# Feed-forward down-projection: which of four column blocks takes the seven-product form, and which one accumulates in PSUM

## The chip, the cores and the metric

The kernel runs on one core of one Trainium2 chip. Its engines work side by side, each through its own list of instructions in order: TensorE (PE; its weight loads are listed as PEld), VectorE (DVE), ScalarE (ACT), GpSimd (POOL), and SyncE (SP), which here only issues DMAs. TensorE writes its products to PSUM; DVE and ACT read them there. The metric is device time in microseconds (us): three runs took 2527.45, 2529.25 and 2530.73 us, median 2529.25.

## The reference

Two decoder layers over 256 positions of width 2048, float32. Each layer has a mixer (layer 0: gated DeltaNet and retention heads, layer 1: gMLP spatial gating) and then a squared-ReLU feed-forward of hidden width 8192. The change touches the feed-forward alone:

```python
def squared_relu_mlp(h, w_up, w_down):
    return jnp.square(jax.nn.relu(h @ w_up)) @ w_down
...
        h = h + rmsnorm(y, norm_w[layer, 1])
        y = squared_relu_mlp(rmsnorm(h, norm_w[layer, 2]), ffn_w_up[layer], ffn_w_down[layer])
        h = h + rmsnorm(y, norm_w[layer, 3])
```

`w_up` is 2048 x 8192 and `w_down` 8192 x 2048. There are two feed-forwards in one execution.

## The kernel before, in words

**Three products for one.** Every float32 operand is split into a rounded part ("hi") and a rest ("lo"), and each matrix product is made of three: hi*hi, lo*hi, hi*lo. Weights arrive by DMA in pieces of 128 x 2048 numbers (1 MB) in a tile `raw`; ACT writes `whi`, DVE subtracts and writes `wlo` (`weights`, L125 and L126; for seven-product blocks `split`, L189 and L190). There are three `raw` buffers and four each of `whi` and `wlo`, used in turn. So the third product of a piece cannot start before DVE has made its `wlo`.

**Groups.** The hidden width is cut into 16 groups of 512. In the loop of `ffn`, group c of the up-projection (`up_pass`: four units of 48 matmuls with 256 columns, L318 to L320, into two `tp` banks) is interleaved with the down-projection of group c-1, whose output is cut into four blocks of 512 columns, block 0 to 3. `ORDER` sets the sequence: unit, block 0, unit, block 1, unit, block 2, unit, block 3; for the first turn of the loop `FIRST` replaces it. After the last unit ACT takes relu and square (L386, L387), and DVE and ACT split the result into `e` (hi and lo) and into sums `f` for the seven-product form (`sums`, L398 to L401). Groups 0 to 14 go through the loop this way; the last one is done by `down_last`.

**Two forms of a down block.** The plain one (`chunk_tok`) is one 1 MB piece of weights, one L125 and one L126 of 128 x 2048, and 24 matmuls with 512 columns (L132 to L134) into two `acc` banks. The seven-product one (`chunk7`, with `mul7`) is Strassen's scheme in Winograd's form on halves: from the same 1 MB, DVE makes sums of quarter blocks in `qsum` (L341 to L343), and two splits follow, one of `raw` (1536 columns) and one of `qsum` (2048 columns). TensorE then runs 42 matmuls with 256 columns (L362 to L364) in this order: 12 into the first `acc` bank and 6 into the first `mx` bank, which need only the split of `raw`, then 12 into the second `acc` bank and 12 into the second `mx` bank, which need the split of `qsum`. DVE adds the four results to `Y["a"]`, `Y["b"]`, `Y["c"]`, `Y["d"]` in SBUF (L424; for the first group a copy, L422). After the loop `combine` puts the parts together, once for each such column block.

**Who does what before the change.** Blocks 0 and 2 take the seven-product form in all 15 groups. Block 1 (`KEPT`) takes it in odd groups only; in even groups it is plain and accumulates in two `acc` banks (`kept`) that stay occupied through the stage, and `combine` adds these. Block 3 is plain in all groups, and DVE adds its two banks to `y` in SBUF each time (L242). Of the eight PSUM banks four are `acc`, two `mx`, two `tp`; with `kept` two `acc` banks are left for the rest.

**What sets the order.** The kernel is written in the order above; the tile framework assigns every instruction to its engine's list and decides, when the program is built, in which order ready work stands there. On the chip each engine keeps that order. The raw loads all go through SP's queue.

Of the kernel before, what the change touches and what calls it, by code (L numbers as in the profile page):

```python
# [13 lines left out]
ALU = mybir.AluOpType  # L14
# [15 lines left out]
PARTS = [4, 2, 1, 1]  # L30
WAIT = [26, 30]
AHEAD = 200
SEVEN, KEPT = (0, 1, 2), 1
ORDER = (None, 0, None, 1, None, 2, None, 3)
FIRST = (None, None, 1, None, 0, None, 3, 2)

C_IDENT, C_TRI, C_NEG, C_M1, C_M2, C_COS, C_SIN = 0, 128, 256, 384, 512, 640, 768
C_END = 896
# [55 lines left out]
def program(tc, nc, A, S):  # L94
# [8 lines left out]
    V, G, ACT, PE, DMA = nc.vector, nc.gpsimd, nc.scalar, nc.tensor, nc.sync  # L103
# [3 lines left out]
    def T(pool, shape, tag, dt=F32, bufs=None):  # L107
        uid[0] += 1
        kw = {} if bufs is None else {"bufs": bufs}
        return pool.tile(shape, dt, tag=tag, name=f"{tag}_{uid[0]}", **kw)  # L110

    def bank(pool, n, tag):
        return T(pool, [P, 512], tag)[:, :n]

    def weights(s, blocks, parts=1):
        src, width = s.take(blocks)
        raw = T(wp, [P, 2048], "raw", bufs=RAW_BUFS)[:, :width]
        hi = T(wp, [P, 2048], "whi", F32R, bufs=HI_BUFS)[:, :width]
        lo = T(wp, [P, 2048], "wlo", F32R, bufs=LO_BUFS)[:, :width]
        with tc.high_priority(offset=ahead[0]):  # L120
            n = width // parts
            for c in range(0, width, n):
                r, a, d = raw[:, c : c + n], hi[:, c : c + n], lo[:, c : c + n]
                DMA.dma_start(r, src[:, c : c + n])
                ACT.activation(a, r, AF.Copy)  # L125
                V.tensor_tensor(d, r, a.bitcast(F32), ALU.subtract)  # L126
        return hi, lo

    def prod_tok(ps, x, b, w, j, n, first, last):
        xh, xl = x[0][:, b * P : (b + 1) * P], x[1][:, b * P : (b + 1) * P]  # L130
        wh, wl = w[0][:, j * n : (j + 1) * n], w[1][:, j * n : (j + 1) * n]
        PE.matmul(ps, xh, wh, start=first, stop=False)  # L132
        PE.matmul(ps, xl, wh, start=False, stop=False)  # L133
        PE.matmul(ps, xh, wl, start=False, stop=last)  # L134
# [7 lines left out]
    def tick():  # L142
        clock[0] += 1
        while queue and queue[0][0] <= clock[0]:
            gen = heapq.heappop(queue)[2]
            delay = next(gen, None)
            if delay is not None:
                spawn(delay, gen)
# [6 lines left out]
    def chunk_tok(s, X, rows, spans, n, ps=None, first=True, last=True):  # L155
        if ps is None:
            ps = [bank(acc, n, "acc") for _ in range(2)]
        for u in range(0, len(rows), 4):
            w = weights(s, [(r, spans) for r in rows[u : u + 4]])
            for j in range(4):  # L160
                k = u + j
                for b in range(2):
                    prod_tok(ps[b], X[k], b, w, j, n, first and k == 0, last and k == len(rows) - 1)
                tick()
        return ps
# [32 lines left out]
    def kts(groups):  # L198
        return [(e[0][:, j, :], e[1][:, j, :]) for e in groups for j in range(4)]
# [37 lines left out]
    def acc_to_y(ps, b, c, first):  # L237
        if first:
            y[b][c] = T(hp, [P, 512], f"y{b}{c}")
            V.tensor_copy(y[b][c], ps)  # L240
        else:
            V.tensor_tensor(y[b][c], ps, y[b][c], ALU.add)  # L242
# [64 lines left out]
    def up_pass(s, X, c, ps):  # L307

        for u in range(4):
            wh, wl = weights(s, [(r, [(c * 512, 512)]) for r in ALLK[u * 4 : u * 4 + 4]])  # L310
            for j in range(4):
                k = u * 4 + j
                xh, xl = X[k]
                for m in range(4):
                    out = ps[m // 2][:, (m % 2) * SEQ : (m % 2 + 1) * SEQ]
                    col = slice(j * 512 + m * P, j * 512 + (m + 1) * P)

                    PE.matmul(out, wh[:, col], xh, start=k == 0 and m % 2 == 0, stop=False, skip_group_check=True)  # L318
                    PE.matmul(out, wh[:, col], xl, start=False, stop=False, skip_group_check=True)  # L319
                    PE.matmul(out, wl[:, col], xh, start=False, stop=k == NKT - 1, skip_group_check=True)  # L320
                tick()
            yield
# [54 lines left out]
    def ffn(up, dn, X, rh, w1i, w0i):  # L377
        last = HID // 512 - 1
        with tc.tile_pool(name=f"ffn{w1i}", bufs=1, reuse_waits="tile") as fp:

            def pair(name):
                return T(fp, [P, 4, SEQ], f"{name}h", F32R), T(fp, [P, 4, SEQ], f"{name}l", F32R)
# [23 lines left out]
            def rows(c):  # L406
                return [c * 512 + j * P for j in range(4)]

            Y, kept = {}, [bank(acc, 512, "acc") for _ in range(2)]
# [6 lines left out]

            def block(c, g, e, f):

                if c in SEVEN and not (c == KEPT and g % 2 == 0):
                    for k, p in zip("abcd", chunk7(dn, fp, e, f, rows(g), c * 512)):  # L420
                        if g == (c == KEPT):
                            V.tensor_copy(Y[k, c], p)  # L422
                        else:
                            V.tensor_tensor(Y[k, c], p, Y[k, c], ALU.add)  # L424
                elif c == KEPT:
                    chunk_tok(dn, kts([e]), rows(g), [(c * 512, 512)], 512, kept, g == 0, g == last - 1)
                else:
                    for b, p in enumerate(chunk_tok(dn, kts([e]), rows(g), [(c * 512, 512)], 512)):
                        acc_to_y(p, b, c, g == 0)

            def combine(c):
                a, b, p, p3 = [Y[k, c] for k in "abcd"]
                u = T(fp, [P, 512], "rl", bufs=3)[:, :256]
                l, r = slice(0, 256), slice(256, 512)
                V.tensor_tensor(u, a[:, l], b[:, l], ALU.add)
                V.tensor_tensor(a[:, l], a[:, l], a[:, r], ALU.add)
                V.tensor_tensor(a[:, r], p[:, l], p3, ALU.add)
                V.tensor_tensor(a[:, r], a[:, r], u, ALU.subtract)
                V.tensor_tensor(u, u, b[:, r], ALU.add)
                V.tensor_tensor(b[:, l], u, p[:, r], ALU.add)  # L440
                V.tensor_tensor(b[:, r], p[:, l], u, ALU.subtract)
                if c == KEPT:
                    V.tensor_tensor(a, kept[0], a, ALU.add)
                    V.tensor_tensor(b, kept[1], b, ALU.add)
                y[0][c], y[1][c] = a, b

            def halves_of(tiles):
# [2 lines left out]
            e = pair("e0")  # L450
# [11 lines left out]
            for c in range(1, last + 1):  # L462
# [4 lines left out]
                todo = up_pass(up, X, c, ps)  # L467
                order = ORDER if c > 1 else FIRST
                for n, o in enumerate(order):
                    if o is None:  # L470
                        next(todo)
                        if None not in order[n + 1 :]:
# [4 lines left out]
                            if c < last:  # L477
                                a = [x.rearrange("p (m b t) -> p b m t", b=2, t=P) for x in r]
# [3 lines left out]
                e, f = e2, f2  # L482
# [666 lines left out]
```

## Time and profile before

| | us |
|---|---|
| median of three runs | 2529.25 (2527.45 to 2530.73) |
| profiled execution, its own time | 2528.85 |
| its span from first to last instruction | 2527.0 |
| PE busy | 2490.6 (99%) |
| DVE busy | 1991.3 (79%) |
| ACT busy | 1249.8 (49%) |
| DMA queue 1 | 475.70 MB, 52.7% of 16 engines |

The two loops over groups lie at about 577 to 1228 us and 1844 to 2490 us of the span. In the rows of the trace a matmul's duration is longer than the distance to the next one, since matmuls overlap; the distance between starts is what a matmul costs. The same holds, to a smaller degree, for DVE and ACT: the row of a 128 x 2048 subtraction says 2.29 us and the next one starts 2.2 us later. L numbers are lines of the kernel before; up to L441 they hold for the changed kernel too.

### The profile page before, as it was taken

Reading aid. Unit: us, or ns where it says so; the run is one execution under the profiler, and the core shown is the slowest. Engines: PE = TensorE matmul, PEld = TensorE weight load, DVE = VectorE, ACT = ScalarE, POOL = GpSimd, SP = SyncE. Lnnn points to the kernel's source line nnn. Section 1 sums busy time; section 2 is a strip of 40 time slices with the busy share of each in tenths; the row PEclk is TensorE's granted clock in tenths of the full one; section 3 lists DMA queues with packets and bytes.
Section 4 is the critical chain, followed back from the end, with each engine's and each line's share of the span. In section 5 each row is a group of like instructions: output and inputs, shape, how many; then the busy total and the mean of one; then the engine's idle time right before and its main releaser. Section 6 shows DMA issues by size and latency. Waiting matters only on the chain.

```text
span 2527.0 us, 37082 instructions
## 1 busy us (share of the span) xinstructions
PE 2490.6 (99%) x15406; PEld 2210.5 (87%) x15406; DVE 1991.3 (79%) x2318; ACT 1249.8 (49%) x1256; POOL 203.6 (8%) x158
## 2 busy tenths in 40 slices
PE   8999999999999999999999999999999999999998
PEld 7778888879999999999878878777799999999997
DVE  7586755578898898889854596866889988988897
ACT  6554444455554555555543433333455545555553
POOL 3000201130000000000210120110300000000001
PEclk9999999999999999999999999999999999999999
DMA  7444544544555555555555455565445555555553
GB/s 248 181 152 148 187 157 175 204 167 175 209 184 195 206 200 184 187 209 207 192 206 185 181 203 189 199 217 200 150 167 200 199 185 209 192 191 189 199 207 131
DMA packets 81256, 478.07 MB, mean 189 GB/s; under 512 B 13632, under 2 KB 15808, under 8 KB 26816
## 3 DMA queue, kind: packets, MB, share of 16 engines
q1 hardware_dynamic: 81088, 475.70, 52.7%
q8 instruction: 121, 1.98, 0.3%
q14 instruction: 47, 0.39, 0.0%
HBM read 473.04 MB, written 2.62 MB: 188 GB/s over the span
## 4 chain that ended last, share of the span: by engine, by line
PE 46%; DVE 3%; POOL 1%; issue 0%; ACT 0%; DVEq 0%; POOLq 0%; ACTq 0%
PE acc L134 8%; PE acc L132 8%; PE acc L133 8%; PE tp L318 4%; PE tp L320 4%; PE tp L319 4%; PE acc L362 1%; PE acc L363 1%; PE acc L364 1%; PE mx L362 1%; PE mx L363 1%; PE mx L364 1%; DVE h L275 1%; DVE wlo L126 1%; PE mx L1059 1%
## 5 line engine op out<-in xcount | busy, mean ns | idle before, releaser
L126 DVE TENSOR_TENSOR wlo<-raw,whi 128x2048 fp32r<-128x2048 f32 (+3 forms) x366 | 828.9, 2267 | 275.1 <-ACT whi L125 273.3
L125 ACT ACTIVATE whi<-raw 128x2048 fp32r<-128x2048 f32 (+3 forms) x366 | 687.1, 1878 | 490.6 <-PE acc L133 313.0
L318 PE MATMUL tp<-xh,whi 128*128 128x256 f32 x1920 | 539.5, 281 | 0.0
L319 PE MATMUL tp<-xl,whi 128*128 128x256 f32 x1920 | 539.2, 281 | 0.0
L320 PE MATMUL tp<-xh,wlo 128*128 128x256 f32 x1920 | 539.1, 281 | 0.0
L132 PE MATMUL acc<-whi,xh 128*128 128x512 f32 (+3 forms) x1120 | 445.4, 398 | 5.8 <-ACT whi L125 5.8
L134 PE MATMUL acc<-wlo,xh 128*128 128x512 f32 (+3 forms) x1120 | 438.8, 392 | 6.8 <-DVE wlo L126 6.8
L133 PE MATMUL acc<-whi,xl 128*128 128x512 f32 (+3 forms) x1120 | 438.5, 391 | 0.0
L318 PEld LDWEIGHTS tp<-xh,whi 128*128 128x128 f32 x1920 | 361.5, 188 | 2.1
L319 PEld LDWEIGHTS tp<-xl,whi 128*128 128x128 f32 x1920 | 361.6, 188 | 1.9
L320 PEld LDWEIGHTS tp<-xh,wlo 128*128 128x128 f32 x1920 | 361.7, 188 | 0.0
L134 PEld LDWEIGHTS acc<-wlo,xh 128*128 128x128 f32 x1120 | 211.3, 189 | 55.0 <-DVE wlo L126 8.8
L132 PEld LDWEIGHTS acc<-whi,xh 128*128 128x128 f32 x1120 | 211.6, 189 | 51.2 <-ACT whi L125 6.0
L133 PEld LDWEIGHTS acc<-whi,xl 128*128 128x128 f32 x1120 | 211.7, 189 | 45.0 <-issue 1.0
L189 ACT ACTIVATE whi<-qsum 128x2048 fp32r<-128x2048 f32 x74 | 142.1, 1920 | 211.4 <-DVE qsum L343 202.1
L190 DVE TENSOR_TENSOR wlo<-qsum,whi 128x2048 fp32r<-128x2048 f32 x74 | 169.5, 2290 | 66.7 <-ACT whi L189 66.7
L189 ACT ACTIVATE whi<-raw 128x1536 fp32r<-128x1536 f32 x74 | 110.5, 1493 | 183.5 <-DMA raw<-dn 73.3
L424 DVE TENSOR_TENSOR y<-acc,y 128x512 f32<-128x512 f32 x136 | 92.3, 686 | 49.7 <-PE acc L364 49.4
L190 DVE TENSOR_TENSOR wlo<-raw,whi 128x1536 fp32r<-128x1536 f32 x74 | 129.7, 1753 | 0.4
L265 POOL TENSOR_TENSOR e0h<-y,f1h 128x512 f32<-128x512 f32 x8 | 13.0, 1648 | 1349.9 <-DVE y L263 1349.9
L133 PE MATMUL acc<-whi,e0l 128*128 128x512 f32 x256 | 101.2, 395 | 0.0
L134 PE MATMUL acc<-wlo,e0h 128*128 128x512 f32 x256 | 101.1, 395 | 0.0
(353 smaller groups left out, 4337.4 us busy)
## 6 DMA issues: line engine op xcount, KB each, us to landing
raw<-up SPq DMA_DIRECT2D x128, 1024.0 KB, 4.8
raw<-dn SPq DMA_DIRECT2D x128, 1024.0 KB, 4.8
raw<-sg_in SPq DMA_DIRECT2D x64, 1024.0 KB, 4.8
raw<-la_in SPq DMA_DIRECT2D x56, 1024.0 KB, 4.8
raw<-sg_out SPq DMA_DIRECT2D x32, 1024.0 KB, 4.8
raw<-la_out SPq DMA_DIRECT2D x16, 1024.0 KB, 4.8
raw<-la_in SPq DMA_DIRECT2D x4, 768.0 KB, 4.7
kq<-xT SPq DMA_DIRECT2D x8, 256.0 KB, 6.4
```

What stands on the lines that cost most here:

```text
L125: ACT.activation(a, r, AF.Copy)
L126: V.tensor_tensor(d, r, a.bitcast(F32), ALU.subtract)
L132: PE.matmul(ps, xh, wh, start=first, stop=False)
L133: PE.matmul(ps, xl, wh, start=False, stop=False)
L134: PE.matmul(ps, xh, wl, start=False, stop=last)
L189: ACT.activation(hi, src, AF.Copy)
L190: V.tensor_tensor(lo, src, hi.bitcast(F32), ALU.subtract)
L318: PE.matmul(out, wh[:, col], xh, start=k == 0 and m % 2 == 0, stop=False, skip_group_check=True)
L319: PE.matmul(out, wh[:, col], xl, start=False, stop=False, skip_group_check=True)
L320: PE.matmul(out, wl[:, col], xh, start=False, stop=k == NKT - 1, skip_group_check=True)
L362: PE.matmul(ps, x[k][0], wh, start=k == 0, stop=False, skip_group_check=True)
L424: V.tensor_tensor(Y[k, c], p, Y[k, c], ALU.add)
```

## The change

`KEPT` becomes block 3. Blocks 0, 1 and 2 now take the seven-product form in all 15 groups. Block 3 stays plain, and accumulates in the two `kept` banks from the first to the last group of the loop; DVE copies these to `y` once, after group 14, so its L242 rows for each group go, and `combine` no longer adds `kept`. In the first turn of the loop block 3 takes the place that block 1 had, and blocks 1 and 2 follow each other at its end.

```diff
-SEVEN, KEPT = (0, 1, 2), 1
+SEVEN, KEPT = (0, 1, 2), 3
 ORDER = (None, 0, None, 1, None, 2, None, 3)
-FIRST = (None, None, 1, None, 0, None, 3, 2)
+FIRST = (None, None, 3, None, 0, None, 1, 2)
...
-                if c in SEVEN and not (c == KEPT and g % 2 == 0):
+                if c in SEVEN:
                     for k, p in zip("abcd", chunk7(dn, fp, e, f, rows(g), c * 512)):
-                        if g == (c == KEPT):
+                        if g == 0:
                             V.tensor_copy(Y[k, c], p)
                         else:
                             V.tensor_tensor(Y[k, c], p, Y[k, c], ALU.add)
-                elif c == KEPT:
+                else:
                     chunk_tok(dn, kts([e]), rows(g), [(c * 512, 512)], 512, kept, g == 0, g == last - 1)
-                else:
-                    for b, p in enumerate(chunk_tok(dn, kts([e]), rows(g), [(c * 512, 512)], 512)):
-                        acc_to_y(p, b, c, g == 0)
+                    if g == last - 1:
+                        for b in range(2):
+                            acc_to_y(kept[b], b, c, True)
...
-                if c == KEPT:
-                    V.tensor_tensor(a, kept[0], a, ALU.add)
-                    V.tensor_tensor(b, kept[1], b, ALU.add)
                 y[0][c], y[1][c] = a, b
```

The build puts the instructions in another order on the engines as well. First, DVE's list at block 2 of a group in the steady part of the loop. Before (an odd group, the one that has three seven-product blocks), where `qsum_6406`, `raw_6405` and `acc_6419` are block 2's:

```order
L341 TENSOR_TENSOR qsum_6406<-raw_6405 128x1024
L190 TENSOR_TENSOR wlo_6409<-raw_6405,whi_6407 128x1536
L424 TENSOR_TENSOR y_887_4619<-acc_6301,y_887_4619 128x512
L424 TENSOR_TENSOR y_888_4620<-acc_6303,y_888_4620 128x512
L424 TENSOR_TENSOR d_883_4615<-mx_6302,d_883_4615 128x256
L342 TENSOR_TENSOR qsum_6406<-qsum_6406,raw_6405 128x512
L424 TENSOR_TENSOR bc_4621<-mx_6304,bc_4621 128x512
L343 TENSOR_TENSOR qsum_6406<-qsum_6406,raw_6405 128x512
L190 TENSOR_TENSOR wlo_6410<-qsum_6406,whi_6408 128x2048
L126 TENSOR_TENSOR wlo_6471<-raw_6469,whi_6470 128x2048
L424 TENSOR_TENSOR y_890_4622<-acc_6419,y_890_4622 128x512
```

(the first four L424 rows add block 1's results). After, where `qsum_5999`, `raw_5998` and `acc_6012` are block 2's:

```order
L341 TENSOR_TENSOR qsum_5999<-raw_5998 128x1024
L190 TENSOR_TENSOR wlo_6002<-raw_5998,whi_6000 128x1536
L342 TENSOR_TENSOR qsum_5999<-qsum_5999,raw_5998 128x512
L343 TENSOR_TENSOR qsum_5999<-qsum_5999,raw_5998 128x512
L424 TENSOR_TENSOR y_890_4622<-acc_6012,y_890_4622 128x512
L190 TENSOR_TENSOR wlo_6003<-qsum_5999,whi_6001 128x2048
L424 TENSOR_TENSOR bc_4614<-mx_6013,bc_4614 128x256
L126 TENSOR_TENSOR wlo_6064<-raw_6062,whi_6063 128x2048
```

What moved: the addition of block 2's first result (`acc_6012`) now stands ahead of the split of the same block's `qsum`. This is so in block 2 of groups 1 to 14 of both feed-forwards, and in block 1 of group 1; before, it was so nowhere.

Second, TensorE's list at the same place, after the 18 matmuls of block 2 that need only the split of `raw`. Before:

```order
L362 MATMUL acc_6421<-whi_6408,f1h_6073 128x256
L363 MATMUL acc_6421<-whi_6408,f1l_6074 128x256
L364 MATMUL acc_6421<-wlo_6410,f1h_6073 128x256
L362 MATMUL acc_6421<-whi_6408,f1h_6073 128x256
L363 MATMUL acc_6421<-whi_6408,f1l_6074 128x256
```

After (`tp_5706` and `tp_5707` are the up-projection's next unit):

```order
L362 MATMUL acc_6014<-whi_6001,f0h_5670 128x256
L363 MATMUL acc_6014<-whi_6001,f0l_5671 128x256
L362 MATMUL mx_6015<-whi_6001,f0h_5670 128x256
L363 MATMUL mx_6015<-whi_6001,f0l_5671 128x256
L318 MATMUL tp_5706<-xh_822_4342,whi_6063 128x256
L319 MATMUL tp_5706<-xl_823_4343,whi_6063 128x256
L318 MATMUL tp_5707<-xh_822_4342,whi_6063 128x256
L319 MATMUL tp_5707<-xl_823_4343,whi_6063 128x256
L364 MATMUL acc_6014<-wlo_6003,f0h_5670 128x256
```

What moved: eight matmuls that read only `whi` stand ahead of the first one that reads `wlo_6003`, four of them of the next unit.

Third, DVE's list where the first turn of the loop ends and the second begins. `wlo_5221` is the weights' split of the second turn's first unit, the L422 rows copy results of blocks 2 of group 0. Before:

```order
L126 TENSOR_TENSOR wlo_5221<-raw_5219,whi_5220 128x2048
L190 TENSOR_TENSOR e1l_4783<-rl_5099,e1h_4782 128x512
L190 TENSOR_TENSOR f1l_5112<-tr_5106,f1h_5111 128x1024
L240 COPY y_957_5147<-acc_5115 128x512
L240 COPY y_958_5149<-acc_5116 128x512
L422 COPY bc_4624<-mx_5168 128x512
```

After, where the same split is `wlo_5249`:

```order
L190 TENSOR_TENSOR wlo_5184<-qsum_5180,whi_5182 128x2048
L190 TENSOR_TENSOR f1l_5112<-tr_5106,f1h_5111 128x1024
L422 COPY y_890_4622<-acc_5193 128x512
L422 COPY y_891_4623<-acc_5195 128x512
L422 COPY bc_4614<-mx_5194 128x256
L422 COPY bc_4624<-mx_5196 128x512
L126 TENSOR_TENSOR wlo_5249<-raw_5247,whi_5248 128x2048
```

What moved: the split for the next unit now stands behind the four copies of block 2's results, the last of which (`mx_5196`) reads what block 2's last matmul writes.

## The prediction

> **What bounds the kernel now.** I read the page's busy shares first, then the two feed-forward loops in stretches of one group each, then TensorE and DVE row by row in those groups.
>
> ```profile
> PE 2490.6 (99%) x15406; PEld 2210.5 (87%) x15406; DVE 1991.3 (79%) x2318; ACT 1249.8 (49%) x1256; POOL 203.6 (8%) x158
> 881.60:924.60 43.00, 43.00 (x343) 41.89 (x342) 40.83 (x43) 21.72 (x17) 0.00 (x0) 1.00 0.49 178
> 924.60:968.30 43.70, 43.70 (x325) 41.50 (x324) 36.06 (x33) 24.60 (x20) 0.00 (x0) 1.00 0.58 211
> 576.90:664.50 87.60, 87.55 (x671) 83.99 (x670) 79.63 (x80) 48.96 (x40) 0.00 (x0) 1.00 0.56 203
> 664.50:1184.70 520.20, 520.20 (x3998) 500.38 (x3998) 460.76 (x446) 275.82 (x210) 0.00 (x0) 1.00 0.55 195
> ```
>
> A row of a stretch gives its length, then busy us of PE, PEld, DVE, ACT, POOL, the granted clock and the DMA share. The first stretch is a group with three seven-product blocks, the second one with two, the third the loop's first two turns, the last twelve turns together. TensorE has no gap in any of them: it is the bound. But DVE is busy 40.83 of 43.00 us in the group with three such blocks, and rests only in the other (36.06 of 43.70). The starts on TensorE say what a block costs:
>
> ```profile
> 902.76 0.28 PE L318 MATMUL tp<-xh,whi 128*128 128x256 f32 x1
> 908.44 0.28 PE L362 MATMUL acc<-whi,e1h 128*128 128x256 f32 x1
> 913.34 0.28 PE L318 MATMUL tp<-xh,whi 128*128 128x256 f32 x1
> 919.01 0.39 PE L132 MATMUL acc<-whi,e1h 128*128 128x512 f32 x1
> 924.61 0.28 PE L318 MATMUL tp<-xh,whi 128*128 128x256 f32 x1
> ```
>
> Unit 5.67 (913.34 to 919.01), seven-product block 4.90 (908.44 to 913.34; 42 matmuls, 0.117 each), plain block 5.60 (919.01 to 924.61; 0.233 each).
>
> **Part 1: the product saved.** Block 1 turns from plain to seven-product in the even groups 0 to 14: 8 per feed-forward, 16 in all. Each takes TensorE 4.90 instead of 5.60: 16 x 0.70 = -11.2 us, if TensorE never waits.
>
> **Part 2: DVE's work.** The prices of its rows, from start to next start:
>
> ```profile
> 928.11 1.22 DVE L190 TENSOR_TENSOR f0l<-tr,f0h 128x1024 fp32r<-128x1024 f32 x1
> 929.25 2.29 DVE L126 TENSOR_TENSOR wlo<-raw,whi 128x2048 fp32r<-128x2048 f32 x1
> 941.22 0.69 DVE L342 TENSOR_TENSOR qsum<-qsum,raw 128x512 f32<-128x512 f32 x1
> 941.95 0.69 DVE L343 TENSOR_TENSOR qsum<-qsum,raw 128x512 f32<-128x512 f32 x1
> 970.78 1.28 DVE L242 TENSOR_TENSOR y<-acc,y 128x512 f32<-128x512 f32 x2
> 971.97 2.28 DVE L126 TENSOR_TENSOR wlo<-raw,whi 128x2048 fp32r<-128x2048 f32 x1
> 986.21 1.76 DVE L190 TENSOR_TENSOR wlo<-raw,whi 128x1536 fp32r<-128x1536 f32 x1
> 987.88 1.28 DVE L424 TENSOR_TENSOR y<-acc,y 128x512 f32<-128x512 f32 x2
> 989.08 0.42 DVE L424 TENSOR_TENSOR d<-mx,d 128x256 f32<-128x256 f32 x1
> 989.41 0.69 DVE L342 TENSOR_TENSOR qsum<-qsum,raw 128x512 f32<-128x512 f32 x1
> 990.61 0.68 DVE L343 TENSOR_TENSOR qsum<-qsum,raw 128x512 f32<-128x512 f32 x1
> 993.36 2.29 DVE L190 TENSOR_TENSOR wlo<-qsum,whi 128x2048 fp32r<-128x2048 f32 x1 [2.07 <-ACT whi L189]
> 995.57 2.29 DVE L126 TENSOR_TENSOR wlo<-raw,whi 128x2048 fp32r<-128x2048 f32 x1
> 1004.31 1.22 DVE L341 TENSOR_TENSOR qsum<-raw 128x1024 f32<-128x1024 f32 x1
> 1005.44 1.75 DVE L190 TENSOR_TENSOR wlo<-raw,whi 128x1536 fp32r<-128x1536 f32 x1
> 1007.11 0.42 DVE L400 TENSOR_TENSOR tr<-rl 128x256 f32<-128x256 f32 x1
> 1007.45 0.69 DVE L342 TENSOR_TENSOR qsum<-qsum,raw 128x512 f32<-128x512 f32 x1
> ```
>
> 2048 columns cost 2.21 (993.36 to 995.57), 1536 cost 1.67, 1024 cost 1.13, 512 cost 0.60, 256 cost 0.34; L343 right behind L342 costs 0.73 (941.22 to 941.95). Every group now has the work of the old odd one less the two L242 additions (1.19): 40.83 - 1.19 = 39.6 us, under TensorE's 43.0. By the sum alone DVE keeps up, and 3.4 us per group are left for its waits. The order decides whether that is enough.
>
> **Part 3: the reversed rows at block 2.** DVE's list now has the addition of the block's own first result ahead of the split of its `qsum`. So DVE cannot make `wlo` before TensorE has run the block's first 12 matmuls, and TensorE needs that `wlo` soon after.
>
> ```profile
> 952.13 0.28 PE L362 MATMUL acc<-whi,e0h 128*128 128x256 f32 x1
> 953.41 0.28 PE L364 MATMUL acc<-wlo,e0h 128*128 128x256 f32 x1
> 953.73 0.69 DVE L424 TENSOR_TENSOR y<-acc,y 128x512 f32<-128x512 f32 x1 [3.02 <-PE acc L364]
> ```
>
> Here DVE waits for the same thing today, harmlessly: its addition starts 1.60 after the block (953.73 - 952.13). With the new order the split follows at 1.60 + 0.60 = 2.20 and is written at 2.20 + 2.29 = 4.49. TensorE meanwhile has 12 + 6 + 4 matmuls of the block and 4 of the next unit: 26 x 0.117 = 3.04. It then waits 4.49 - 3.04 = 1.45, with some hundredths for the signal 1.5 us. The four of the next unit need a `whi` that ACT writes behind the `qsum` one; that falls inside the same wait. Block 2 of groups 1 to 14, two feed-forwards: 28 x 1.5 = +42.0. Behind the waiting addition on DVE are the next unit's split, block 3's and the next turn's first, so this delay does not shorten anything later. Bounds: 1.45 is a fixed chain of rows; only a DVE that comes still later makes it more.
>
> **Part 4: once round the group.** From that split's end to the split of the next group's block 1, DVE has, in its new order: 0.34, 2.21, two additions 1.20, block 3's and the next unit's splits 4.42, L341 and 1536 columns 2.80, the activations' splits and sums 2 x 0.60 + 4 x 0.34 = 2.56, L342 and L343 1.33, `f` 1.14, block 0's `qsum` split 2.21, a unit's 2.21, block 0's additions 2.14, L341 1.13, L342 0.60, 1536 columns 1.67, L343 0.60: 26.6. To these come waits for ACT's `whi` of a `qsum`: the row at 993.36 shows 2.07 where nothing stands between, at block 1; at block 0 `f` (1.14) stands between, leaving 1.0; I add 0.3 for the first splits after relu. With the last split's 2.29: 26.6 + 2.07 + 1.0 + 0.3 + 2.29 = 32.3. TensorE in the same time: the rest of block 2, 20 x 0.117 = 2.33; the rest of the unit 5.20; block 3 5.60; unit 5.67; block 0 4.90; unit 5.67; the first 20 matmuls of block 1 2.33: 31.7, plus 0.14 since it resumed that much after DVE went on. It waits 32.3 - 31.84, about 0.4 us, at block 1 of groups 2 to 14: 26 x 0.4 = +10.4. Bounds: 0 if ACT's waits come out half a us shorter, 1.3 if the splits after relu wait for the whole of both relus (0.9 more).
>
> **Part 5: the first two turns.** The split for the second turn's first unit now stands behind the copy of block 2's last result. After that block ends DVE needs about 0.2 + 0.60 + 2.29 = 3.1; TensorE has four more matmuls, 0.47: 2.6 per feed-forward, +5.2. Group 1's block 1 has the reversed rows too: 2 x 1.5 = +3.0. Bounds for both feed-forwards: 5 (the first alone), and 16, if blocks 1 and 2 of group 0, which run with no unit between, and each unit of the second turn wait too (8.0 per feed-forward in place of 4.1): DVE's 79.63 in these two turns grows by the difference of a seven-product and a plain kept block, 1.13 + 1.20 + 1.67 + 2.14 = 6.1, less 2.4 for L242 and its first copies, to 83.3 of 86.9.
>
> **Costed at nothing.** The two copies after group 14 replace the two additions in `combine`: 1.2 us of DVE on either side, at the same place. The raw loads keep their sizes and their count; SP's list differs at a few places only. A second pair of `acc` banks does not come free: two stay kept, as before. At the end of the loop DVE comes later than before by up to a us or two, covered by the 96 matmuls of `down_last`; if that cover is gone, 2 x 2 us.
>
> **The sum.** -11.2 + 42.0 + 10.4 + 5.2 + 3.0 = +49.4. Against the profiled execution: span 2527.0 + 49.4 = 2576, own time 2528.85 + 49.4 = 2578. The median, 2529.25, is 0.4 above that time: forecast 2579 us, 2.0% slower.
>
> **Rivals.** *First, the gain arrives* (the other side): DVE is early enough everywhere, TensorE stays full, 2529.25 - 11.2 = 2518. For it: the old odd groups carry more DVE work (40.83) with no gap. Against: there the `qsum` split stood ahead of the addition, and the new list cannot be run that way. It decides if TensorE's list had 13 more matmuls (1.5 / 0.117) at that place that need no `wlo`; it has four.
>
> *Second, DVE and ACT become the bound of the whole group*: if each of the three `qsum` splits waits 2.07 for ACT and the addition waits for TensorE as well (3.02 in the row above), a group takes 39.6 + 6.2 + up to 1.6 = 47, against (43.0 x 7 + 43.7 x 8) / 15 = 43.4 now. 28 x 3.6 = +101, with part 5 some 2638. For it: DVE's room is only 3.4 us. Against: at block 0 `f` fills half of the wait, and at block 2 the addition does, so the waits overlap.
>
> *Third, the clock falls.* If after each gap TensorE ran some us at half speed, say 1.7 us lost each time, 56 gaps would cost another 95: 2674.
>
> ```profile
> 1222.70:1275.00 52.30, 47.85 (x216) 36.99 (x216) 46.81 (x73) 31.10 (x55) 26.63 (x17) 1.00 0.51 195
> ```
>
> In this stretch, between the loop and the next mixer, TensorE rests 52.30 - 47.85 = 4.45 us in pieces, at a granted clock of 1.00; in a group the change would leave 1.9 of 45. [...]
>
> **How the numbers follow.** The forecast's case has 0.80, the first rival 0.07, the second 0.10, the third 0.03. The case's own bounds: part 4 at 0 and part 5 at 5: 2529.25 - 11.2 + 42.0 + 5 = 2565; part 4 at 1.3 (33.8) and part 5 at 16: 2529.25 - 11.2 + 42 + 33.8 + 16 = 2610. I take 2557 to 2610: the lower end gives 8 us for a wait at block 2 of 1.2 in place of 1.5. Two runs of this kernel differ by about 0.1%, so 0.2% is what can be told from no change: 2524 to 2534. Faster 0.07 is the first rival; same 0.03 is left for a case where block 2's wait is a quarter of its size; slower 0.90.
>
> **What would show it.** Stretches of one group in the steady loop: 44.9 us instead of 43.00 and 43.70, with TensorE about 43 busy and DVE about 39.6. In the waits: PE's L364 on DVE's `wlo` L190 (or its L318 on ACT's `whi`, the same wait), 28 times 1.5, and DVE's L424 on PE ahead of `wlo`. Part 4 is wrong if block 1 shows no gap or one over 1.3; part 5 if the gap before the second turn's unit is not about 2.6. The prediction is wrong as a whole if TensorE shows no gap at block 2, or if the clock in the stretches is under 1.00.

## The result, and the profile after

The change makes the kernel slower: median 2599.53 us (2596.51 to 2602.45) against 2529.57 us, a ratio of 1.0278 (95% interval 1.0266 to 1.0290). The forecast was 2579 us with a range of 2557 to 2610. The profiled execution took 2602.45 us with a span of 2600.7, 73.7 more than the span before, where the sum said 49.4.

The busy shares of the changed kernel, from its page:

```profile
PE 2512.7 (97%) x15694; PEld 2232.0 (86%) x15694; DVE 2059.4 (79%) x2386; ACT 1257.1 (48%) x1272; POOL 202.9 (8%) x158
```

TensorE has more instructions than before (a seven-product block counts 42 smaller ones in place of 24) and less of the span. The stretches show where the time went: one steady group, the first two turns of the loop, twelve turns, and the last turn with `down_last` up to the next transposes (columns as in the prediction):

```profile
719.03:764.05 45.02, 43.84 (x344) 42.21 (x342) 40.07 (x39) 23.48 (x18) 0.00 (x0) 1.00 0.52 187
578.93:673.97 95.04, 89.30 (x690) 85.10 (x688) 82.23 (x83) 46.83 (x39) 0.00 (x0) 1.00 0.49 179
673.97:1216.45 542.48, 526.01 (x4106) 506.66 (x4105) 482.19 (x467) 280.12 (x216) 0.00 (x0) 1.00 0.52 187
1216.45:1284.70 68.25, 62.20 (x411) 55.70 (x410) 60.17 (x75) 32.64 (x31) 4.96 (x5) 0.97 0.55 206
```

Of the kernel before, the row that answers to the last of these:

```profile
1184.67:1246.92 62.25, 60.20 (x395) 54.17 (x393) 52.24 (x65) 30.74 (x28) 5.69 (x5) 1.00 0.58 212
```

| first feed-forward, us | before | after | difference | by the sum of the prediction |
|---|---|---|---|---|
| first two turns | 87.60 | 95.04 | 7.4 | 4.9 |
| twelve turns | 520.20 | 542.48 | 22.3 | 18.6 |
| last turn and `down_last` | 62.25 | 68.25 | 6.0 | 1.2 |
| sum | 670.05 | 705.77 | 35.7 | 24.7 |

(The last column spreads the parts of the prediction: -0.70 in each even group; 1.5 at block 2 and 0.4 at block 1 of each group from 2 on; for the first two turns 2.6 + 1.5 + 1.5 - 0.7.) The second feed-forward loses about as much. 2 us more lie ahead of the first loop, where the kernels do the same; the other profiled executions of this record reach that loop between 574.7 and 578.1 us, so we take these 2 us for chance.

At block 2 of a steady group these are the rows of DVE, ACT and TensorE in the changed kernel that matter here (others stand between them):

```profile
926.09 0.69 DVE L343 TENSOR_TENSOR qsum<-qsum,raw 128x512 f32<-128x512 f32 x1
926.89 1.92 ACT L189 ACTIVATE whi<-qsum 128x2048 fp32r<-128x2048 f32 x1 [7.72 <-DVE qsum L343]
928.35 0.69 DVE L424 TENSOR_TENSOR y<-acc,y 128x512 f32<-128x512 f32 x1 [1.57 <-PE acc L364]
928.72 5.50 ACT L125 ACTIVATE whi<-raw 128x2048 fp32r<-128x2048 f32 x3
928.95 2.28 DVE L190 TENSOR_TENSOR wlo<-qsum,whi 128x2048 fp32r<-128x2048 f32 x1
929.33 0.28 PE L363 MATMUL mx<-whi,f1l 128*128 128x256 f32 x1
930.67 0.39 PE L318 MATMUL tp<-xh,whi 128*128 128x256 f32 x1 [1.05 <-ACT whi L125]
```

DVE's addition (L424) waits for TensorE, and then TensorE, which has come to the next unit, waits for a `whi`. ACT begins that one at 928.72 (the first of the three in its row), right behind the `whi` of the block's `qsum`, which it could begin only when DVE's L343 had ended: the addition does not stand in this chain. From 929.33 to 930.67 are 1.34 us where 0.117 is the pitch, 1.22 lost; three matmuls around it, each the first to read a tile just written, take 0.1 more (this L318 is one, 0.39 in place of 0.28). That is 1.53 us, where the prediction had 1.5. But the waits of DVE, grouped over the twelve turns, show a larger item, which the prediction counted only in passing:

```profile
L190 DVE TENSOR_TENSOR wlo<-qsum,whi 128x2048 fp32r<-128x2048 f32 x36 | 82.4, 2289 | 34.8 <-ACT whi L189 34.8
L424 DVE TENSOR_TENSOR y<-acc,y 128x512 f32<-128x512 f32 x72 | 49.4, 686 | 18.7 <-PE acc L364 18.7
```

34.8 / 12 = 2.9 us of a group DVE waits for ACT to write the `whi` of a `qsum`, 1.56 for TensorE.

### The profile page after: what moved, and what is told of

It reads as the page before. It is cut to its first block, busy times and chain, and to the rows that moved or that the text cites. A ratio compares the mean times of both kernels' runs of the same rounds, so it can differ in the third digit from the quotient of the medians.

```text
span 2600.7 us, 37748 instructions
## 1 busy us (share of the span) xinstructions
PE 2512.7 (97%) x15694; PEld 2232.0 (86%) x15694; DVE 2059.4 (79%) x2386; ACT 1257.1 (48%) x1272; POOL 202.9 (8%) x158
## 4 chain that ended last, share of the span: by engine, by line
PE 29%; DVE 12%; ACT 4%; issue 3%; DMA 1%; POOL 1%; ACTq 0%; DVEq 0%; POOLq 0%
PE acc L132 7%; PE acc L134 7%; PE acc L133 7%; DVE wlo L190 3%; ACT whi L189 3%; DVE wlo L126 2%; PE tp L318 2%; PE tp L320 2%; PE tp L319 2%; DMA raw<-dn 1%; DVE y L424 1%; ACT whi L125 1%; DVE h L275 1%; PE acc L364 1%; DVE qsum L343 1%
## 5 line engine op out<-in xcount | busy, mean ns | idle before, releaser
L126 DVE TENSOR_TENSOR wlo<-raw,whi 128x2048 fp32r<-128x2048 f32 (+3 forms) x350 | 789.9, 2266 | 256.5 <-ACT whi L125 255.3
L125 ACT ACTIVATE whi<-raw 128x2048 fp32r<-128x2048 f32 (+3 forms) x350 | 649.1, 1870 | 364.0 <-PE acc L133 285.6
L318 PE MATMUL tp<-xh,whi 128*128 128x256 f32 x1920 | 540.4, 283 | 32.0 <-ACT whi L125 32.0
L320 PE MATMUL tp<-xh,wlo 128*128 128x256 f32 x1920 | 530.4, 281 | 4.9 <-DVE wlo L126 4.8
L318 PEld LDWEIGHTS tp<-xh,whi 128*128 128x128 f32 x1920 | 362.2, 189 | 39.7 <-ACT whi L125 38.3
L189 ACT ACTIVATE whi<-qsum 128x2048 fp32r<-128x2048 f32 x90 | 172.9, 1922 | 456.7 <-DVE qsum L343 308.4
L190 DVE TENSOR_TENSOR wlo<-qsum,whi 128x2048 fp32r<-128x2048 f32 x90 | 206.0, 2289 | 82.0 <-ACT whi L189 82.0
L133 PEld LDWEIGHTS acc<-whi,xl 128*128 128x128 f32 x1120 | 212.6, 190 | 44.9 <-issue 1.0
L190 DVE TENSOR_TENSOR wlo<-raw,whi 128x1536 fp32r<-128x1536 f32 x90 | 158.0, 1756 | 10.7 <-ACT whi L189 10.5
L424 DVE TENSOR_TENSOR y<-acc,y 128x512 f32<-128x512 f32 x168 | 115.3, 686 | 47.3 <-PE acc L364 47.3
L189 ACT ACTIVATE whi<-raw 128x1536 fp32r<-128x1536 f32 x90 | 133.3, 1481 | 23.6 <-PE tp L319 11.8
L341 DVE TENSOR_TENSOR qsum<-raw 128x1024 f32<-128x1024 f32 x90 | 109.8, 1220 | 6.3 <-DMA raw<-dn 6.1
L386 ACT ACTIVATE rl<-tp 128x512 f32<-128x512 f32 x60 | 35.5, 592 | 129.7 <-PE tp L320 129.7
```

Of the source, the lines that this page charges most:

```text
L189: ACT.activation(hi, src, AF.Copy)
L190: V.tensor_tensor(lo, src, hi.bitcast(F32), ALU.subtract)
L341: V.tensor_tensor(Q[:, 0:2, :], B[:, 1:3, :], B[:, 0:1, :].to_broadcast([P, 2, 512]), ALU.add)
```

## The question, and the theories

Was it the reversed rows that cost the time? Three readings were set against each other.

- **A**: DVE's whole round is too long. Its work of some 40 us a group and its waits for ACT's `whi` of the three `qsum` exceed TensorE's 43.0. What counts is whether other work stands in those waits, whichever row it is.
- **B**, the prediction as written: the reversed rows cost 1.5 us each by themselves.
- **C**: three seven-product blocks are too much work for DVE in any order.

In DVE's rows of the changed kernel the three waits are:

```profile
903.35 2.29 DVE L190 TENSOR_TENSOR wlo<-qsum,whi 128x2048 fp32r<-128x2048 f32 x1 [0.85 <-ACT whi L189]
...
913.29 0.69 DVE L343 TENSOR_TENSOR qsum<-qsum,raw 128x512 f32<-128x512 f32 x1
916.03 2.29 DVE L190 TENSOR_TENSOR wlo<-qsum,whi 128x2048 fp32r<-128x2048 f32 x1 [2.05 <-ACT whi L189]
```

0.85 at block 0, 2.05 at block 1 (DVE's last sum ends, ACT rounds for 1.92 us, DVE subtracts), and at block 2 the place of that wait is taken by the addition that waits for TensorE.

## Experiments: the order on DVE

**Reversed rows undone.** The additions of a seven-product block are queued behind the split of its own `qsum` (`qlo[0]` is that split; `issue_after` puts what stands under it behind the named instruction):

```diff
+        with tc.issue_after(qlo[0].ins):
+            for k, p in zip("abcd", parts):
+                (V.tensor_copy(Y[k, c], p) if g == 0 else
+                 V.tensor_tensor(Y[k, c], p, Y[k, c], ALU.add))
```

> Edit: the changed kernel, with the additions of every seven-product block (L424, L422) queued on DVE behind the split of the same block's qsum. Nothing else is changed; the reversed rows at block 2 are gone. Theory A (DVE's waits for ACT): the reversed row only fills a wait that DVE has anyway while ACT writes the whi of qsum (2.05 us after L343); with the addition behind it, DVE stands idle there, and a steady group stays at 45.0 to 45.4 us: 2599 to 2612 us. Theory B (the prediction as written: the reversed row is what costs 1.5 us at block 2): the 28 waits of 1.5 go, 2599.5 - 42 = 2558 us, steady group 43.5. Theory C (DVE has too much work whatever its order): 2599, group 45.0.

Measured: 2617.99 us, ratio 1.0351 (1.0336 to 1.0367): slower still. Twelve turns of it:

```profile
672.23:1222.42 550.19, 530.97 (x4106) 507.98 (x4104) 481.63 (x467) 278.75 (x215) 0.00 (x0) 1.00 0.51 184
```

Its groups of DVE's rows in the same stretch:

```profile
L190 DVE TENSOR_TENSOR wlo<-qsum,whi 128x2048 fp32r<-128x2048 f32 x36 | 82.5, 2293 | 59.6 <-ACT whi L189 59.6
L424 DVE TENSOR_TENSOR y<-acc,y 128x512 f32<-128x512 f32 x72 | 48.2, 684 | 0.0
```

The wait of the addition is gone (0.0), and the wait for ACT has grown from 34.8 to 59.6: block 2's `qsum` now waits its full 2.07. So B falls. From L343's start to the split's start DVE takes 2.86 us in the changed kernel, with the addition between them (926.09 to 928.95 above), and 2.75 here, with nothing between (927.85 to 930.60): the reversed row delays the split by 0.1 us, not by 1.5. TensorE's wait at block 2 is still there, and ends on the same `whi`:

```profile
932.42 0.39 PE L318 MATMUL tp<-xh,whi 128*128 128x256 f32 x1 [1.06 <-ACT whi L125]
```

The reversed row did not make the loss; it stood in a wait that was there without it. Taken out of that wait, the addition's 0.6 us is added to the group (45.8 us for 45.2).

**The waits filled.** In all blocks the split of `raw` (1536 columns, 1.67 us of DVE) is queued behind the last sum, so that it stands between that sum and the split which needs ACT's answer:

```diff
-        V.tensor_tensor(Q[:, 3, :], Q[:, 2, :], B[:, 3, :], ALU.add)
-        split(hi[0][:, :1536], lo[0][:, :1536], raw[:, 512:])
+        q3 = V.tensor_tensor(Q[:, 3, :], Q[:, 2, :], B[:, 3, :], ALU.add)
+        with tc.issue_after(q3.ins): split(hi[0][:, :1536], lo[0][:, :1536], raw[:, 512:])
```

> Edit: the changed kernel, with one more edge on DVE: the split of raw (1536 columns, 1.67 us) is queued behind L343, so it stands in the time in which ACT writes the whi of qsum. The work is the same. Theory A: the three waits of a group (about 2.05, 0.85 and the 1.57 before the reversed row) go, DVE's 39.6 us fit in 43.0, and TensorE has no gap in the steady groups (43.0 us each): 28 times about 2.0 and some of the extra at the first turns and at the end of the loop go, 2518 to 2527 us. Theory B: the reversed row goes as well in this order, so 2558 us and a second gap of 0.4 stays at block 1. Theory C: 2599.

Measured: 2525.09 us (2523.77 to 2528.09), ratio 0.9983 (0.9973 to 0.9992). Twelve turns:

```profile
669.48:1185.45 515.97, 515.97 (x4105) 502.78 (x4104) 488.91 (x472) 289.28 (x220) 0.00 (x0) 1.00 0.56 199
```

Its groups of DVE's rows in the same stretch:

```profile
L190 DVE TENSOR_TENSOR wlo<-qsum,whi 128x2048 fp32r<-128x2048 f32 x37 | 84.6, 2286 | 2.5 <-ACT whi L189 2.2
L424 DVE TENSOR_TENSOR y<-acc,y 128x512 f32<-128x512 f32 x72 | 48.5, 685 | 22.0 <-PE acc L364 22.0
```

TensorE has no gap, a group takes 515.97 / 12 = 43.0, and DVE now waits for TensorE (22.0) and hardly for ACT (2.2). C falls: the work is the same. The twelve turns are 4.2 us shorter than before the change (520.20), which is six blocks by 0.70: part 1's saving arrives whole once DVE is on time.

The same edit in the kernel before:

> Edit: the kernel before, with the same one edge on DVE (split of raw behind L343). Theory A: TensorE had no gap in the loops of the kernel before, so filling DVE's wait gives nothing: 2525 to 2530 us; the distance to the changed kernel with the same edge is then what the saved products give, 11.2 us by the sum. If the edge alone speeds up something else: under 2524.

Measured: 2529.08 us, ratio 1.0001 (0.9992 to 1.0010). In this kernel TensorE had no gap in the loops, and the order is worth nothing.

**One block at a time.** The edit at block 0 alone, then at block 1 and at block 2 alone (the `with` stands under `if col // 512 == 0`, `== 1`, `== 2`).

> The changed kernel, with the split of 1536 columns of raw queued behind the block's last qsum sum at block 0 only; blocks 1 and 2 keep the changed kernel's order. Theory A (threshold): DVE's 39.6 us of a group and its waits for ACT's whi of the qsum (0.85 at block 0, 2.05 at block 1, 1.57 at block 2, together about 4.5) exceed TensorE's 43.0 by about 1.1 to 2, and it is that excess which appears as gaps; filling the wait at block 0 alone (0.85, and what its piece waits for behind it) takes away most of it, so that block 1's gap of 0.4 and most of block 2's 1.55 go: 2525 to 2560 us, steady group 43.0 to 44.2. Theory D (each wait counts by itself, where it stands): block 2's gap of 1.55 stays, since nothing was altered there, and only block 1's 0.4 and its bumps go: 2599 - 26 x 0.4 - 2 x 4 = about 2580, steady group 44.5 or more.

> The changed kernel with the split of 1536 columns queued behind the sums at block 1 only, where DVE's wait for ACT is the longest (2.05). Theory A (one sum of work and waits against TensorE's 43.0): up to 1.67 of the 2.05 is filled, more than at block 0 (0.85), where it sufficed: steady group 43.0 to 43.6, 2531 to 2560. If the place counts and block 0 is the one that matters: steady group about 45, 2590 to 2600.

> The same at block 2 only, where the reversed rows are: the split of 1536 columns then stands between the last sum and the split of the qsum, and covers the wait that the addition covered before. Theory A: the wait for the addition (1.57) is filled in part, steady group 43.0 to 44.0, 2531 to 2570. If the place counts and block 0 is the one that matters: about 45, 2590 to 2600. If the reversed rows were the cause after all, this and no other single place should reach fill's 2525.

Measured: block 0 alone 2531.67 us (ratio 1.0013, 1.0003 to 1.0023), block 1 alone 2573.96 (1.0171, 1.0154 to 1.0188), block 2 alone 2576.48 (1.0184, 1.0168 to 1.0199). The first is as theory A said; the other two are in neither range. Twelve turns of block 1 alone:

```profile
672.24:1202.13 529.89, 520.50 (x4105) 504.73 (x4104) 481.57 (x464) 278.80 (x216) 0.00 (x0) 1.00 0.53 191
```

Its groups of DVE's rows in the same stretch:

```profile
L190 DVE TENSOR_TENSOR wlo<-qsum,whi 128x2048 fp32r<-128x2048 f32 x36 | 82.5, 2292 | 39.1 <-ACT whi L189 39.1
```

The wait for ACT is larger than in the changed kernel, 39.1 against 34.8. DVE's rows say why. An edit at one block makes the scheduler write the others in another order as well. With the edit at block 1, the additions at block 2 went behind the split, and this wait opened there:

```profile
962.26 0.69 DVE L343 TENSOR_TENSOR qsum<-qsum,raw 128x512 f32<-128x512 f32 x1
965.02 2.29 DVE L190 TENSOR_TENSOR wlo<-qsum,whi 128x2048 fp32r<-128x2048 f32 x1 [2.07 <-ACT whi L189]
```

With the edit at block 0, additions of ready results and the split of `raw` came to stand in the wait at block 1 too, without being asked:

```profile
905.01 0.69 DVE L343 TENSOR_TENSOR qsum<-qsum,raw 128x512 f32<-128x512 f32 x1
905.62 0.68 DVE L424 TENSOR_TENSOR y<-acc,y 128x512 f32<-128x512 f32 x1
...
906.55 1.75 DVE L190 TENSOR_TENSOR wlo<-raw,whi 128x1536 fp32r<-128x1536 f32 x1
908.22 0.68 DVE L424 TENSOR_TENSOR y<-acc,y 128x512 f32<-128x512 f32 x1
908.82 2.28 DVE L190 TENSOR_TENSOR wlo<-qsum,whi 128x2048 fp32r<-128x2048 f32 x1
```

So these three runs do not price one place each, as they were meant to; they are three more lists of DVE, and the version filled at all blocks is another. What they can be compared by is DVE's idle time. A group is always DVE's busy and idle time together, and the busy time is nearly the same in all of them (40.1 to 40.7). So the groups differ by the idle time, and by what ends it: the longer the waits in the last two columns are together, the longer is the group (to within 0.1 us), and TensorE is full where almost all of the idle time is a wait for TensorE (per group, from the stretches and groups of each kernel):

| DVE's list | group | DVE busy | idle | of it for ACT's `whi` of `qsum` | for TensorE at L424 |
|---|---|---|---|---|---|
| changed kernel | 45.2 | 40.2 | 5.0 | 2.9 | 1.6 |
| reversed rows undone | 45.8 | 40.1 | 5.7 | 5.0 | 0 |
| filled at block 1 | 44.2 | 40.1 | 4.0 | 3.3 | 0 |
| filled at block 2 | 44.3 | 40.1 | 4.2 | 3.1 | 0 |
| filled at block 0 | 43.0 | 40.7 | 2.3 | 0.1 | 1.9 |
| filled at all blocks | 43.0 | 40.7 | 2.3 | 0.2 | 1.8 |

## Experiments: the first turn, a pure reversed row, more work

**Another order of the first turn**, with the filled waits and then in the changed kernel alone:

```diff
-FIRST = (None, None, 3, None, 0, None, 1, 2)
+FIRST = (None, None, 3, 0, None, 1, None, 2)
```

> Edit: as the one before, and the first turn of the loop runs in the order unit, unit, block 3, block 0, unit, block 1, unit, block 2, so that no two seven-product blocks stand next to each other. Theory A with part 5 of the prediction right (2.6 us and more at the first turns come from the copies of block 2 ahead of the next unit's split): 2.5 to 4 us per feed-forward less than without it, 2513 to 2521 us. If the first turn's extra lies elsewhere (activations that are late there): the same time as without it.

> The changed kernel with another order of the loop's first turn alone (up-projection units between the seven-product blocks of group 0, no other edit). With the raw split queued behind the sums in all blocks the same order of the turn gave 2525.1 - 2515.4 = 9.7 us. If the first turns' loss stands by itself, as part 5 of the prediction has it: 2599.5 - 9.7 = about 2590, steady group 45.0 as before. If it is the same lateness of DVE, which a better first turn only hands on to the third turn: 2597 to 2602.

Measured: with the filled waits 2515.44 us (2514.81 to 2516.51), ratio 0.9946 (0.9931 to 0.9961), half a per cent faster than the kernel before; alone 2586.75 us (2586.02 to 2587.71), ratio 1.0225 (1.0210 to 1.0240). The gains are 9.7 and 12.8 us, near enough to call the first turns' loss one of its own, as part 5 has it. In the profiled executions 9.3 and 11.4 us of them lie in the first two turns of the two feed-forwards; why the second gain is larger is not explained. The first two turns, with the filled waits and this order:

```profile
574.70:661.87 87.17, 87.08 (x689) 84.48 (x688) 82.80 (x84) 48.73 (x41) 0.00 (x0) 1.00 0.54 195
```

87.17 us against 95.04 in the changed kernel and 87.60 before.

**The reversed row where DVE is otherwise on time.** In the fastest version the addition of block 2's first result is put ahead of the split of its `qsum`, in groups 1 to 14:

```diff
+            ev = add(pa)
+            with tc.issue_after(ev.ins): V.tensor_tensor(lo1, q, hi1.bitcast(F32), ALU.subtract)
```

> The fastest version so far (the raw split behind the qsum sums in all blocks, and another order of the first turn), with the prediction's reversed rows put back by force at block 2 of groups 1 to 14 alone: the addition of the block's own first result ahead of the split of its qsum. Here DVE is otherwise in time, so the prediction's part 3 stands by itself: 4.49 us from block start to the qsum's wlo; TensorE's list at that place has 22 matmuls of the block, 4 of the next unit (26 x 0.117 = 3.04) and then 4 of block 3 with 512 columns (0.93), 3.97 in all. If part 3's chain is right: a gap of about 0.5 at block 2 of 28 groups, 2515.4 + 28 x 0.52 = about 2530 (2526 to 2540). If the reversed rows cost nothing where DVE is in time: 2515 to 2518. If they cost the full 1.5 each: 2557.

Measured: 2551.71 us (2551.50 to 2552.56), above the 2526 to 2540 of the first case and below the 2557 of the third. The addition is L425 here and its split L374. Eleven turns:

```profile
707.17:1189.73 482.56, 478.12 (x3764) 460.85 (x3762) 440.20 (x428) 254.89 (x199) 0.00 (x0) 1.00 0.53 193
```

Rows of its timeline at one block 2:

```profile
911.09 0.69 DVE L425 TENSOR_TENSOR y<-acc,y 128x512 f32<-128x512 f32 x1 [3.29 <-PE acc L364]
911.70 2.28 DVE L374 TENSOR_TENSOR wlo<-qsum,whi 128x2048 fp32r<-128x2048 f32 x1
914.03 0.39 PE L364 MATMUL acc<-wlo,f1h 128*128 128x256 f32 x1 [0.42 <-DVE wlo L374]
```

The block begins at 909.49, so the addition starts 1.60 after it, the split ends at 4.49 and TensorE goes on at 4.54: part 3's chain to the hundredth, with DVE idle for 3.29 ahead of it. TensorE is 0.58 late by its starts, where 0.52 was expected. Not expected were the restarts of about 0.1 us, again at matmuls that read a tile just written (this L364 is one, 0.39 in place of 0.28): a group takes 482.56 / 11 = 43.87, 0.87 more than 43.0, and 28 x 0.87 = 24 us. Of the other 12 us, 5 lie behind the twelve turns of the first feed-forward, 3.6 of them in `down_last`, and 6 behind those of the second. So the reversed row has a price where DVE is on time; in the changed kernel the wait for ACT covered it. From the loop's end to the transposes, this kernel:

```profile
1229.39:1257.11 27.72, 21.76 (x89) 15.58 (x87) 23.29 (x41) 13.12 (x18) 4.98 (x5) 1.00 0.61 240
```

And the fastest version:

```profile
1215.19:1239.30 24.11, 22.17 (x94) 16.94 (x93) 20.09 (x39) 11.36 (x17) 5.67 (x5) 1.00 0.57 223
```

**More work for DVE.** In the fastest version a sum of the `qsum` is done a second time, which writes the same numbers again: in the first run the one of 512 columns, in the second the one of 1024 columns as well.

```diff
+        V.tensor_tensor(Q[:, 2, :], Q[:, 0, :], B[:, 2, :], ALU.add)
+        V.tensor_tensor(Q[:, 0:2, :], B[:, 1:3, :], B[:, 0:1, :].to_broadcast([P, 2, 512]), ALU.add)
```

> The fastest version so far, with the qsum's second sum (512 columns) done twice in every seven-product block: 0.60 to 0.73 more DVE work, three times a group, about 2 us, and the same result. DVE's work of a group becomes 41.6 of TensorE's 43.0. If the waits are filled, as theory A says, work up to 43.0 is free: no gap in the steady group, 2515 to 2525 us, the little more at the first turns and the end. If what is left of waits is over 1.4 us a group, it shows by the rest: each 0.1 us over 43.0 gives 28 x 0.1 = 2.8 us, at most 28 x 2 = +56.

> As the run before, with the qsum's first sum (1024 columns) done twice as well: about 1.13 + 0.65 = 1.8 more per block, 5.3 us a group; DVE's work becomes 44.9, over TensorE's 43.0. Theory A: DVE is now the bound, steady group 44.9 and what is left of waits (up to 1.5): 2515 + 28 x 1.9 = 2568 at the least, 2610 at the most. If DVE's work did not set the group: 2515 to 2525.

Measured: 2551.32 us (2550.87 to 2554.72), not free, and 2677.34 us (2673.72 to 2682.04), more than the 2610 that was the most. Twelve turns of the first:

```profile
666.61:1190.59 523.98, 523.09 (x4105) 506.30 (x4104) 506.72 (x500) 280.10 (x215) 0.00 (x0) 1.00 0.53 193
```

Its groups of DVE's rows in the same stretch:

```profile
L190 DVE TENSOR_TENSOR wlo<-qsum,whi 128x2048 fp32r<-128x2048 f32 x36 | 82.4, 2289 | 9.4 <-ACT whi L189 9.4
```

Eleven turns of the second:

```profile
673.77:1200.72 526.95, 491.52 (x3763) 472.82 (x3762) 507.25 (x497) 255.69 (x198) 0.00 (x0) 0.98 0.48 176
```

The sums used for both expectations were too small. DVE is busy 506.72 / 12 = 42.2 us a group in the first, not 41.6, and 507.25 / 11 = 46.1 in the second, not 44.9. They start from part 2's 39.6, but the filled version has 40.7 without any added row: its sums stand one right behind the other, and a row that needs the one ahead of it starts later (0.73 in place of 0.60 in part 2's list). The waits that are left, 1.4 and 1.8 a group, come on top and make groups of 43.7 and 47.9 us. So 1.5 us of added work cost 0.7 a group, and 5.4 cost 4.9. Only 0.5 to 0.8 us of DVE's time was free, not the 3.4 of part 2, and beyond that each us of DVE is about a us of the group: theory A's direction, with a much smaller room.

## Why the prediction was right, point by point

**Part 1** (-0.70 a block) is shown by the filled version: -4.2 in six even groups. With the other first turn as well, the profiled span is 13.3 us shorter than that of the kernel before (2513.7 against 2527.0), 2.2 of them ahead of the first loop, where both do the same: the 11.2 of part 1 arrive. In the changed kernel the waits hide them.

**Part 2** (39.6 us of DVE, TensorE 43.0, room 3.4, "the order decides") named the right balance, with too large a room. DVE was busy 40.2, and the late starts of dependent rows took more of it. What was not done is to add the waits to the work: with those measured for `qsum` and for the addition (0.85, 2.05 and 1.57) 40.2 makes 44.7, over TensorE's 43.0, and the small waits for other answers bring it to the 45.2 of the group.

**Part 3** had the size and not the cause. The loss at block 2 was 1.53 (1.5 predicted), and the chain of 4.49 is confirmed by the reversed row put back alone. But the step "with the new order ... it then waits" failed as a cause: with the rows undone the time rose to 2617.99, since DVE then waits 2.07 for ACT at the same place. "Behind the waiting addition ... this delay does not shorten anything later" was the weak sentence. The addition's wait ran during ACT's work on the same `qsum`, and took the place of a wait as long; the split would have started only 0.1 us earlier without it. The second rival says as much ("at block 2 the addition does"), but part 3 did not use it.

**Part 4** was right as long as the group is regular: TensorE loses 0.40 at block 1, as said (0.41 from 917.97 to 918.38 and 0.22 to the next start, each in place of 0.117), with the waits at block 0 and 1 as assumed (0.85 for 1.0, 2.05 for 2.07). In three of the twelve turns a group was longer, up to 45.88, because a weight piece landed late:

```profile
939.98 1.23 DVE L341 TENSOR_TENSOR qsum<-raw 128x1024 f32<-128x1024 f32 x1 [0.61 <-DMA raw<-dn]
```

That piece was issued at 933.80 and landed at 939.89, after 6.1 us; the one in the group before took 4.7 (888.76 to 893.43). DVE was ready for them 5.6 and 5.5 us after the issue, so this piece was not issued later. Why it took longer to land is not shown, and a fourth `raw` buffer, which might let the loads start earlier, was not tried. The 22.3 us of the twelve turns are 20.0 from regular groups (12 x 45.02 less 520.20) and 2.2 from these.

**Part 5** was too small: 7.4 us for the first two turns where 4.9 was summed. The gap of 2.6 is there, and its cause is the one named:

```profile
621.36 0.39 PE L364 MATMUL acc<-wlo,f0h 128*128 128x256 f32 x1 [0.42 <-DVE wlo L190]
626.95 0.39 PE L320 MATMUL tp<-xh,wlo 128*128 128x256 f32 x1 [2.42 <-DVE wlo L126]
634.89 0.39 PE L318 MATMUL tp<-xh,whi 128*128 128x256 f32 x1 [0.34 <-ACT whi L125]
```

The smaller ones ahead of it and behind it (0.42, 0.34, and more in this turn) were what the upper bound of part 5 stood for.

**"Costed at nothing"** is where the largest part was missed: the last turn and `down_last` of the first feed-forward lost 6.0 us instead of 1.2. From the second one's last turn to the end of the program the loss is 5.4 (80.7 us against 75.3). Together that is about 9 of the 24 us between the sum and the profiled span. "Covered by the 96 matmuls" did not hold: DVE reaches this stage late. TensorE's rows there:

```profile
1268.36 0.50 PE L132 MATMUL acc<-whi,e1h 128*128 128x512 f32 x1 [1.37 <-ACT whi L125]
1270.37 0.65 PE L134 MATMUL acc<-wlo,e1h 128*128 128x512 f32 x1 [1.27 <-DVE wlo L126]
```

The first gap ends with a `whi` whose piece of weights landed at 1266.29; it was issued at 1257.46, just when DVE ended its last splits of the loop (1252.94 to 1257.43). The second ends with a split that DVE begins at 1268.03, behind 3.6 us of copying and combining (from 1264.48). The price given for the loss of that cover, 2 x 2 us, was near (the last turn itself took about 1 us more, and the clock another 1.7, below). The judgement that the cover held was wrong.

**The rivals.** The gain that arrives (2518) was not this kernel's, and "the new list cannot be run that way" was right: another list runs at 2525, and with another first turn at 2515. DVE and ACT as the bound of the whole group, at a chance of 0.10, is the mechanism that the experiments bear out; only its price of 47 us a group was too high, since some waits are covered. The forecast was near because part 3 and part 4 together followed the same round of DVE to its last link and so found its shortfall (1.9 us a group, 2.0 measured in a regular one), though they blamed one row for most of it. That the time stayed inside the range is partly luck: the upper end, 2610, was left for larger waits in parts 4 and 5, and nearly half of the 24 us that came on top of the sum came elsewhere (9 in the last turns, 2 ahead of the first loop).

## What to carry to other kernels

When an engine that waits for another's answer has work near the bound's, add its waits to its work for a whole round and compare that with the bound; a row that waits may only be standing in a wait that was there anyway, and undoing it then gains nothing. To win the time back, put independent work between a request and the use of its answer: here 1.67 us of splitting behind the last sum of each block, with the order that the build made of it, was worth 74 us, without one instruction less. And look at the seams (first turn, end of loop): an engine that runs late in the loop arrives late there, where the cover is thinner.

## What the runs showed of the hardware

The clock fell after short gaps, but not after each. In the filled version, around the gap in the first turns:

```profile
623.15:625.55 2.40, 0.00 (x1) 0.00 (x0) 2.40 (x3) 0.00 (x0) 0.00 (x0) 0.89 0.01 3
625.50:628.00 2.50, 2.43 (x11) 2.43 (x12) 2.43 (x4) 0.00 (x0) 0.00 (x0) 0.50 0.53 125
628.50:631.00 2.50, 2.50 (x24) 2.50 (x23) 2.12 (x2) 2.50 (x2) 0.00 (x0) 1.00 0.60 243
```

In the changed kernel, around a gap as long at the same place:

```profile
624.50:627.00 2.50, 0.08 (x2) 0.05 (x1) 2.50 (x3) 0.00 (x0) 0.00 (x0) 1.00 0.01 3
627.00:630.00 3.00, 3.00 (x25) 3.00 (x26) 3.00 (x3) 0.00 (x0) 0.00 (x0) 1.00 0.61 205
```

And in the version with the most work for DVE, two gaps of the same length, one group apart:

```profile
703.15:705.10 1.95, 0.00 (x0) 0.00 (x0) 1.91 (x2) 1.60 (x1) 0.00 (x0) 1.00 0.02 4
705.50:708.50 3.00, 3.00 (x16) 3.00 (x16) 3.00 (x3) 3.00 (x2) 0.00 (x0) 0.50 0.68 262
...
751.85:753.80 1.95, 0.00 (x0) 0.00 (x0) 1.91 (x2) 1.59 (x1) 0.00 (x0) 1.00 0.00 0
754.00:757.00 3.00, 3.00 (x26) 3.00 (x26) 2.85 (x3) 3.00 (x3) 0.00 (x0) 1.00 0.69 221
```

With a gap of 1.95 to 2.4 us came a stretch at half clock (0.50), or none. In the changed kernel two such stretches lie in the feed-forwards, from 1270.56 to 1273.98 and from 1929.32 to 1932.76 (by windows of 0.02 us), 3.4 us each. Each such stretch costs about half its length, 1.7 us; this is an estimate, from the 11 matmuls in 2.50 us at half clock against 24 in the same time after it, both in the filled version. The changed kernel's gaps of 1.2 us in the steady loop never did this (1.00 in the twelve turns); it has such a fall in `down_last`, behind the two gaps of 1.3 shown above:

```profile
1271.00:1273.50 2.50, 2.50 (x8) 1.91 (x7) 2.50 (x3) 0.00 (x0) 0.00 (x0) 0.50 0.80 272
```

The stretch from 1929.32 lies in the first turns of the second feed-forward, in a gap of the same 2.42 us as the one at 626.95, which had no fall. So the prediction's third rival was real at a smaller size: two such falls, about 3.4 us in all. Its 1.7 us for each gap is half the length of a fall in the kernel before, from 248.52 to 251.96, ahead of the first loop:

```profile
249.00:252.00 3.00, 3.00 (x8) 2.33 (x8) 0.82 (x3) 1.91 (x1) 0.00 (x0) 0.51 0.00 0
```

In the steady group, where that rival was placed, it did not come. Gaps of one length came with a fall and without one (1.95 in the version with the most work for DVE, 2.42 in the changed kernel), and what decides it is not shown by any run here.
